# Two modulation groups of the first layer moved from TensorE to VectorE in a two-layer mLSTM / window-attention encoder

## The chip, the cores and the metric

One core of a Trainium2 chip runs the whole program. The metric is the device time of one execution in microseconds; the median of a few timed runs is what is compared. Beside it stands one profiled execution, from which all shares and durations below are read. TensorE (PE) does matrix products, VectorE (DVE) and ScalarE (ACT) elementwise work, GpSimd (POOL) some elementwise work, and SyncE (SP) issues nearly all transfers.

## What is computed

Two sequences, of 256 and 512 rows with 1024 features each, go through two layers and a final norm. Each layer first makes a modulation vector for each sequence, 6 x 1024 numbers, from that sequence's conditioning vector `c`:

```python
mod = jax.nn.silu(c) @ adaln_w[l] + adaln_b[l]
sh1, sc1, g1, sh2, sc2, g2 = [t[:, None, :] for t in jnp.split(mod, 6, axis=-1)]
h = rmsnorm(x, norm_g[l, 0]) * (1 + sc1) + sh1
y = mlstm_mixer(h, ...)            # layer 0;  swa_mixer in layer 1
x = x + g1 * y
h = rmsnorm(x, norm_g[l, 1]) * (1 + sc2) + sh2
x = x + g2 * conv_ffn(h, ...)
```

The mLSTM mixer of layer 0 has 4 heads. Each head projects queries, keys and values (256 wide each), forms decayed scores in both time directions, and sums values by them. An output gate (a sigmoid of a fourth projection) multiplies the heads' results before the output projection.

## The kernel before

**Layout.** Features lie on partitions, the 768 rows of both sequences along the free axis. Products are kept accurate by splitting each operand into a high and a low float32r part (ScalarE casts the high part, VectorE subtracts for the low part, `fp_copy_split`, L271 to L279), and taking three products (`whi` with `zh`, `whi` with `zl`, `wlo` with `zh`).

**Loads.** A weight piece of 128x1024 numbers (512 KB) is fetched by SyncE into one of 5 rotating buffers called `raw` (L282 to L285), in one queue in order. ScalarE and VectorE make `whi` and `wlo` from it, three buffers each. The matrices for the modulation pass through the same 5 `raw` buffers.

**The order on each engine** is made when the program is built: the instructions are traced in the order of the Python code, and a scheduler with a model of the time puts them in a fixed order for each engine, by that order and by when their inputs are expected. It is not changed at run time: an engine whose next instruction waits does nothing else.

**The modulation.** Layer 0's 48 chunks of 128 numbers are called columns 0 to 47 here, layer 1's are columns 48 to 95; eight columns make a group of 1024 numbers.

- Groups 0 and 1 of layer 0 are made on TensorE at the very start (`adaln`, L418).
- Groups 2 to 5 of layer 0 are made on TensorE in the heads' shadow by `adaln_g` (L479): 8 loads of 512 KB, 32 small fp32 matrix products in four bursts of 8 (`silc`, 32 columns wide, is the moving side's partner; the products of one burst use four column strips of the array), one VectorE and one ScalarE copy, two transposes, two VectorE adds of the bias, and for group 4 two VectorE operations that make the gain. It is a generator with 8 stops (`yield`) in each group.
- All 48 columns of layer 1 are made on VectorE by `adaln_v` (L521), from the transposed matrix `adaln_t`: for each column one load of 512 KB, and for each of the two sequences one multiply-and-sum over 128x1024 numbers (L538), which the profile shows as an instruction named CUSTOM_DVE_ANT_0 and a short read of the sum. It is a generator with one stop before the first column and one after each column; the next column's load is issued one step early.

**Who steps the generators.** `first` (L1720) puts the four `adaln_g` in `self.fillp` and `adaln_v` in `self.fill`, and `mlstm` (L664) steps them between its own instructions with `self.step` (L306). `fillp` is stepped in heads 1, 2 and 3 only: after each of the 4 weight pieces of queries and keys (L768), after rows tiles 1, 3 and 5 of the values (L783), and twice ahead of each sequence's output products (L850): 4 + 3 + 4 = 11 times a head, 33 in all. `fill` is stepped 3 times in head 0 (L781), 6 + 3 times in head 1, 8 + 3 times in each of heads 2 and 3 (L765, L781), and 16 times in the loop of the output gate behind the heads (L892): 50 in all.

**The stretch in question** is from the second half of head 2 to the end of the gate's loop. In each head TensorE does four projections for queries and keys, the scores, the values' projection (`gemmN`, L349), and the output products (L859 to L867); the gate's loop (L885 to L896) is 16 projections. Behind it stand the output projection (`out_proj`, L604) and the feed-forward layer, which read layer 0's groups 2 to 5; layer 1 reads its own columns hundreds of microseconds later.

Of the kernel before, what the change touches and what calls it, by code (L numbers as in the profile page):

```python
# [16 lines left out]
P = 128  # L17
D = 1024
# [163 lines left out]
class Net:  # L182
# [122 lines left out]

    def step(self, gen, n=1):  # L306
        for _ in range(n):
            next(gen, None)

    def gemmT(self, w, q):  # L310

# [206 lines left out]
                    self.cst(NG + (2 * l + i) * 8, 8), ALU.add, ALU.mult,  # L518
                )

    def adaln_v(self, l, pool):  # L521

        nc = self.nc
        stt = nc.vector.scalar_tensor_tensor
        row = pool.tile([P, 2, 1024], F32, name="crow")
        nc.sync.dma_start(row, self.crow.to_broadcast([P, 2, 1024]))
        junk = pool.tile([P, 1024], F32, name="junk")
        mod = self.mod[l]
        fetch = lambda j: self.raw(self.io["adaln_t"][j])
        nxt = fetch(0)  # L530
        yield
        for j in range(48):
            w, nxt = nxt, fetch(j + 1) if j < 47 else None
            with ExitStack() as order:
                if j == 0:
                    order.enter_context(self.tc.issue_after(self.opened.ins))
                for s in range(2):
                    nc.vector.tensor_tensor_reduce(  # L538
                        out=junk, in0=w, in1=row[:, s], scale=1.0, scalar=self.cst(AB + 48 * l + j),
                        op0=ALU.mult, op1=ALU.add, accum_out=mod[:, j, s : s + 1],  # L540
                    )
            i = {15: 0, 39: 1}.get(j)
            if i is not None:
                for s in range(2):
                    stt(
                        self.gain[l][i][:, :, s], mod[:, j - 7 : j + 1, s], 1.0,
                        self.cst(NG + (2 * l + i) * 8, 8), ALU.add, ALU.mult,
                    )
            yield
# [54 lines left out]
    def out_proj(self, u0, act, xt, l, apply):  # L604
# [21 lines left out]
        if not self.begun:  # L626
            first = [next(todo) for _ in range(2)]
            todo = chain(first, todo)
            for i, (z, c, w) in enumerate(first):
                self.product(self.bank[2 + i][:, :H], w, act, 0, H, range(KC - 1))  # L630
                self.begun[i] = KC - 1
# [268 lines left out]
    def opening(self, xt, gw, raws, sinks):  # L900
# [73 lines left out]
        with self.tc.manual_schedule(engines={eng.PE, eng.Activation, eng.DVE}):  # L974
# [36 lines left out]
            def first(c):  # L1011
# [3 lines left out]
                return t  # L1015

            ts = {0: first(0)}
            for c in range(KC):
                if c + 1 < KC:
# [418 lines left out]
    def head(self, u0, last_tile, pool, urows, mark, early):  # L1438
# [64 lines left out]
        def factor():  # L1503
            step()
            wc[1], low = split(ra[1])
            late.append(low)
# [3 lines left out]
        next(first)  # L1510
        late.pop()()
        second = self.outset(pa(), wa[1], rows[1][0], step)
        next(second)
        next(first, None)
        step()
        third = self.outset(pa(), ahead[0], urows[1][:, 0])
        next(third)
# [202 lines left out]
    def first(self, pool):  # L1720

        x = self.io["x"]
        xt = self.load_x(x, RANGES[:1])
        ada = self.adaln(0, 0)
        steps = lambda n: [next(ada, None) for _ in range(n)]
        Norm(self, xt, RANGES[0], self.scaled).run()
        steps(4)
        self.load_x(x, RANGES[1:2], xt)
        steps(2)
        Norm(self, xt, RANGES[1], self.scaled).run()  # L1730
        narrow = self.stg.tile([P, 1024], F32, tag="raw", name=self.nm("raw"), bufs=5)[:, : 16 * KC]
        self.nc.sync.dma_start(narrow, self.io["wg"])
        steps(2)
        gates = [self.stg.tile([P, 1024], R, tag=t, name=self.nm(t), bufs=3) for t in ("whi", "wlo")]
        for t in gates:
            self.nc.gpsimd.memset(t.bitcast(F32), 0.0)
        hi, lo = (t.rearrange("p (j m) -> p j m", m=32)[:, :, 0:4] for t in gates)
        self.fp_copy_split(hi, lo, narrow.rearrange("p (j m) -> p j m", m=4))
        self.fillp = chain(*(self.adaln_g(0, grp) for grp in range(2, 6)))
        self.fill = self.adaln_v(1, pool)  # L1740
        act = self.mlstm(pool, gates, xt)
        for _ in chain(self.fillp, self.fill):
            pass
        return act
# [5 lines left out]
def _colpack(a):  # L1750

    a = a.reshape(a.shape[:-1] + (-1, P))
    return np.moveaxis(a, -1, 0).reshape(P, -1)


def _unit_T(w):

    return w.reshape(KC, P, 2, P).transpose(1, 2, 0, 3).reshape(P, 2048)


def _unit_N(w):

    return w.reshape(KC, P, 256).transpose(1, 0, 2).reshape(P, 2048)


def _unit_D(w):

    return w.reshape(2, P, 2, 512).transpose(1, 2, 0, 3).reshape(P, 2048)
# [14 lines left out]
def _shape_constants():  # L1783
    kc = np.zeros((P, NKC), np.float32)
    kc[:, ID : ID + P] = np.eye(P, dtype=np.float32)
    s = np.arange(P)[:, None]
    t = np.arange(P)[None, :]
    kc[:, MF : MF + P] = np.where(s > t, BIG, 0.0)
    kc[:, MB : MB + P] = np.where(s < t, BIG, 0.0)
    b = _buckets()  # L1790
    kc[b, OH + 510 - np.arange(511)] = 1.0
    rel = 255 - np.arange(511)
    kc[32, OH : OH + 511] = np.where(np.abs(rel) > WINDOW, -BIG, 0.0)
    return kc


def _pack(inp):
    arr = {}
    xs = np.concatenate([inp["x_prompt"][0], inp["x_sample"][0]], axis=0)
    arr["x"] = np.ascontiguousarray(xs.T.reshape(KC, P, T).transpose(1, 0, 2))  # L1800
    cst = np.zeros((P, NCST), np.float32)
    cst[:, NG : NG + 32] = _colpack(inp["norm_g"])
    cst[:, AB : AB + 96] = _colpack(inp["adaln_b"])
    cw = inp["ffn_conv_w"].reshape(DEPTH, 3, 44, P)
    cst[:, CW : CW + 264] = cw.transpose(3, 0, 2, 1).reshape(P, 264)
    cst[:, CB : CB + 88] = _colpack(inp["ffn_conv_b"])
    cst[:, HG : HG + 8] = _colpack(inp["mlstm_head_g"].reshape(1, D))
    cst[:, FG : FG + 8] = _colpack(inp["final_g"])
    cst[:, SK : SK + 16] = inp["attn_sink"][0][None, :]
    bg = inp["mlstm_b_gate"][0].reshape(2, 2, 4)  # L1810
    for d in range(2):
        for ty in range(2):
            cst[32 * d : 32 * d + 4, BG + ty] = bg[d, ty]
    c = np.stack([inp["c_sample"][0], inp["c_prompt"][0]], axis=1)
    cst[:, CT : CT + 16] = c.reshape(KC, P, 2).transpose(1, 0, 2).reshape(P, 16)
    arr["cst"] = cst
    arr["kc"] = _shape_constants()
    w = np.empty((N_UNITS, P, 2048), np.float32)
    wi = inp["mlstm_w_in"][0]
    for h in range(4):  # L1820
        for i in range(3):
            f = _unit_N if i == 2 else _unit_T
            w[U_MIN + 3 * h + i] = f(wi[:, i * D + h * 256 : i * D + (h + 1) * 256])
        w[U_MIN + 12 + h] = _unit_T(wi[:, 3 * D + h * 256 : 3 * D + (h + 1) * 256])
    wg = wi[:, 4 * D :].reshape(D, 2, 2, 4).transpose(0, 2, 1, 3).reshape(KC, P, 16)
    arr["wg"] = np.ascontiguousarray(wg.transpose(1, 0, 2).reshape(P, KC * 16))
    wa = inp["attn_w_in"][0]
    w[U_AIN] = _unit_T(wa[:, 1024:1280])
    w[U_AIN + 1] = _unit_N(wa[:, 1280:1536])
    for u in range(4):  # L1830
        cs = slice(u * 256, (u + 1) * 256)
        w[U_AIN + 2 + u] = _unit_T(wa[:, cs])
        w[U_MOUT + u] = _unit_T(inp["mlstm_w_out"][0][:, cs])
        w[U_AOUT + u] = _unit_T(inp["attn_w_out"][0][:, cs])
    for l in range(DEPTH):
        for p in range(NPART):
            u = U_FFN + (l * NPART + p) * 3
            w[u] = _unit_T(inp["ffn_w_up"][l][:, p * 256 : (p + 1) * 256])
            w[u + 1] = _unit_T(inp["ffn_w_up"][l][:, FF + p * 256 : FF + (p + 1) * 256])
            w[u + 2] = _unit_D(inp["ffn_w_down"][l][p * 256 : (p + 1) * 256])  # L1840
    arr["w"] = w
    arr["adaln_w"] = np.ascontiguousarray(inp["adaln_w"][:1])
    arr["adaln_t"] = np.ascontiguousarray(inp["adaln_w"][1].T).reshape(48, P, D)
    arr["crow"] = np.ascontiguousarray(c.T.reshape(16, P))
    arr["rel_bias"] = np.ascontiguousarray(inp["rel_bias"])
    return arr
# [25 lines left out]
```

## Time and profile before

| what | before |
|---|---|
| median of 3 timed runs | 1807.8 us (1804.55 to 1808.11) |
| the profiled execution, its own time | 1808.25 us |
| its span in the trace | 1806.4 us |
| granted TensorE clock in it | 0.996 |
| ScalarE busy | 887.8 us (49%) |
| GpSimd busy | 488.2 us (27%) |
| HBM read | 176.77 MB |

The span is from the first to the last instruction of the program; the 1.85 us between it and the execution's own time lie around it. A TensorE product is shown with its latency: in a run of products of 256 columns each lasts 0.28 us, and the next begins 0.12 us later, so products overlap in the trace and TensorE looks busy wherever one follows another. What it can be made to do faster is read from the distance of the starts.

### The profile page before, as it was taken

Reading aid. Unit: us, or ns where it says so; the run is one execution under the profiler, and the core shown is the slowest. Engines: PE = TensorE matmul, PEld = TensorE weight load, DVE = VectorE, ACT = ScalarE, POOL = GpSimd, SP = SyncE. Lnnn points to the kernel's source line nnn. Section 1 sums busy time; section 2 is a strip of 40 time slices with the busy share of each in tenths; the row PEclk is TensorE's granted clock in tenths of the full one; section 3 lists DMA queues with packets and bytes.
Section 4 is the critical chain, followed back from the end, with each engine's and each line's share of the span. In section 5 each row is a group of like instructions: output and inputs, shape, how many; then the busy total and the mean of one; then the engine's idle time right before and its main releaser. Section 6 shows DMA issues by size and latency. Waiting matters only on the chain.

```text
span 1806.4 us, 28907 instructions
## 1 busy us (share of the span) xinstructions
PE 1773.1 (98%) x11206; PEld 1644.4 (91%) x11206; DVE 1384.8 (77%) x2219; ACT 887.8 (49%) x1789; POOL 488.2 (27%) x397
## 2 busy tenths in 40 slices
PE   7999999999999999999999999999999999999998
PEld 4988888889998999999999999889989999999997
DVE  4876777895799778777777867767998777777877
ACT  4544433444565444444444657665564444444443
POOL 3000000031024333333331313320144333333323
PEclk9999999999999999999999999999999999999999
DMA  9344665656212222222223331234122222222212
GB/s 360 98 140 135 196 207 180 215 180 219 71 59 71 62 67 71 70 71 71 67 64 94 106 93 42 60 92 138 48 82 71 71 71 71 70 70 71 70 36 71
DMA packets 64997, 185.08 MB, mean 102 GB/s; under 512 B 6247, under 2 KB 24839, under 8 KB 64732
## 3 DMA queue, kind: packets, MB, share of 16 engines
q1 hardware_dynamic: 64284, 182.72, 31.3%
q8 instruction: 88, 1.44, 0.3%
q10 hardware_dynamic: 576, 0.52, 0.1%
q14 instruction: 49, 0.40, 0.1%
HBM read 176.77 MB, written 6.44 MB: 101 GB/s over the span
## 4 chain that ended last, share of the span: by engine, by line
PE 87%; DVE 5%; DMA 3%; ACT 3%; issue 1%; POOL 1%; SPq 0%; DVEq 0%; ACTq 0%; POOLq 0%
PE ps L269 28%; PE pa L269 24%; PE ps L1350 11%; PE ps L1351 10%; PE ps L1353 10%; DMA raw<-in_adaln_t_dram 1%; PE pa L1189 1%; DVE junk L538 1%; DMA slab<-in_adaln_w_dram 1%; DVE wlo L276 1%; PE pa L1350 0%; PE pa L1351 0%; PE pa L1353 0%; ACT zh L1301 0%; DMA raw<-in_adaln_w_dram 0%
## 5 line engine op out<-in xcount | busy, mean ns | idle before, releaser
L275 ACT CAST whi<-raw 128x1024 fp32r<-128x1024 f32 (+1 forms) x231 | 241.0, 1045 | 339.0 <-PE pa L269 144.4
L276 DVE TENSOR_TENSOR wlo<-raw,whi 128x1024 fp32r<-128x1024 f32 (+1 forms) x231 | 312.6, 1354 | 119.1 <-ACT whi L275 116.8
L269 PE MATMUL pa<-slab,whi 128*128 128x256 f32 (+1 forms) x1280 | 307.6, 335 | 0.0
L269 PEld LDWEIGHTS pa<-slab,whi 128*128 128x128 f32 x1280 | 222.2, 188 | 21.6 <-DVE slab L602 0.4
L602 DVE SCALAR_TENSOR_TENSOR slab<-pa,mod,slab 128x256 f32<-128x256 f32 (+1 forms) x320 | 187.2, 603 | 62.7 <-PE pa L269 62.6
L269 PE MATMUL pa<-slab,wlo 128*128 128x512 f32 (+1 forms) x640 | 205.7, 334 | 0.0
L269 PE MATMUL ps<-zh,whi 128*128 128x256 f32 (+1 forms) x560 | 188.1, 337 | 0.3 <-ACT zh L948 0.3
L269 PE MATMUL ps<-zl,whi 128*128 128x256 f32 (+1 forms) x560 | 183.6, 330 | 0.5 <-DVE zl L563 0.5
L269 PE MATMUL ps<-zh,wlo 128*128 128x256 f32 (+1 forms) x560 | 181.7, 330 | 0.0
L1350 PE MATMUL ps<-zh,whi 128*128 128x384 f32 x504 | 172.6, 342 | 3.8 <-ACT nt L1421 2.0
L269 PE MATMUL ps<-slab,whi 128*128 128x384 f32 (+2 forms) x704 | 172.0, 329 | 0.9 <-DVE slab L276 0.5
L1351 PE MATMUL ps<-zl,whi 128*128 128x384 f32 x504 | 169.9, 337 | 0.8 <-DVE zl L1307 0.8
L1353 PE MATMUL ps<-zh,wlo 128*128 128x384 f32 x504 | 169.1, 336 | 0.0
L538 DVE CUSTOM_DVE_ANT_0 junk<-raw,crow,cstt 128x1024 f32<-128x1024 f32 x96 | 125.2, 1305 | 25.1 <-DMA raw<-in_adaln_t_dram 24.5
L1386 POOL TENSOR_TENSOR raw<-raw,raw 128x512 f32<-128x512 f32 x40 | 53.8, 1344 | 319.4 <-DVE wlo L276 246.3
L269 PEld LDWEIGHTS pa<-slab,wlo 128*128 128x128 f32 x640 | 120.4, 188 | 13.2 <-DVE wlo L276 0.4
L1602 POOL TENSOR_TENSOR slab<-slab 128x772 f32<-128x772 f32 x44 | 86.5, 1969 | 163.7 <-DVE slab L1590 150.5
L1589 DVE SCALAR_TENSOR_TENSOR slab<-slab,cstt,slab 128x771 f32<-128x771 f32 x88 | 105.4, 1200 | 26.5 <-ACT slab L1587 26.4
L269 PEld LDWEIGHTS ps<-slab,whi 128*128 128x128 f32 x704 | 122.5, 188 | 3.4 <-ACT whi L275 0.9
L269 PEld LDWEIGHTS ps<-zh,whi 128*128 128x128 f32 x560 | 106.8, 191 | 12.8 <-issue 3.5
L269 PEld LDWEIGHTS ps<-zl,whi 128*128 128x128 f32 x560 | 106.8, 191 | 9.5 <-DVE zl L563 0.7
L269 PE MATMUL ps<-slab,wlo 128*128 128x384 f32 (+2 forms) x352 | 114.8, 328 | 0.1
(301 smaller groups left out, 4286.8 us busy)
## 6 DMA issues: line engine op xcount, KB each, us to landing
raw<-in_w_dram SPq DMA_DIRECT2D x208, 512.0 KB, 3.7
raw<-in_adaln_t_dram SPq DMA_DIRECT2D x48, 512.0 KB, 4.2
raw<-in_adaln_w_dram SPq DMA_DIRECT2D x36, 512.0 KB, 4.5
slab<-in_x_dram SPq DMA_DIRECT2D x12, 512.0 KB, 7.2
slab<-in_adaln_w_dram SPq DMA_DIRECT2D x11, 512.0 KB, 9.2
slab<-mrows SPq DMA_DIRECT2D x8, 384.0 KB, 6.3
xs<-slab SPq DMA_DIRECT2D x6, 512.0 KB, 3.6
bt<-brow SPq DMA_DIRECT2D x16, 192.0 KB, 3.1
```

Of the source, the lines that this page charges most:

```text
L269: self.nc.tensor.matmul(out, lhsT, rhs, start=start, stop=stop)
L275: nc.scalar.copy(hi, src)
L276: return nc.vector.tensor_tensor(lo, src, hi.bitcast(F32), ALU.subtract)
L538: nc.vector.tensor_tensor_reduce(out=junk, in0=w, in1=row[:, s], scale=1.0, scalar=self.cst(AB + 48 * l + j), op0=ALU.mult, op1=ALU.add, a ...
L602: return self.nc.vector.scalar_tensor_tensor(x, o, self.mod[l][:, gc + c, q : q + 1], x, ALU.mult, ALU.add)
L1189: nc.tensor.transpose(pp[:, ks], b.t[:, e, ks], self.ident)
L1350: mm(o, wh[:, k], hi[k], start=start and k == 0, stop=False, skip_group_check=True)
L1351: mm(o, wh[:, k], lo[k], start=False, stop=False, skip_group_check=True)
L1353: mm(o, wl[:, k], hi[k], start=False, stop=k == 3, skip_group_check=True)
L1386: tt(q[0], q[2], q[0], ALU.subtract)
L1589: stt(y[:, 1:], u[:, :-1], w(0), y[:, 1:], ALU.mult, ALU.add)
L1602: nc.gpsimd.tensor_tensor(y, y, yrow[:, j], ALU.mult)
```

## The change

`adaln_v` takes a list of columns of both layers instead of a layer. It now makes columns 48 to 63 (layer 1's first two groups), then 32 to 47 (layer 0's last two groups), then 64 to 95. `fillp` keeps the two `adaln_g` of groups 2 and 3. A step that finds `fillp` at its end steps `fill` instead. The packed transposed matrix holds both layers (on the host, before the run); columns 32 to 47 are loaded from it, and not as groups 4 and 5 from the other matrix.

```diff
     def step(self, gen, n=1):
         for _ in range(n):
-            next(gen, None)
+            if next(gen, self) is self and gen is self.fillp:
+                next(self.fill, None)
...
-    def adaln_v(self, l, pool):
+    def adaln_v(self, columns, pool):
...
-        mod = self.mod[l]
-        fetch = lambda j: self.raw(self.io["adaln_t"][j])
+        fetch = lambda i: self.raw(self.io["adaln_t"][columns[i]])
         nxt = fetch(0)
         yield
-        for j in range(48):
-            w, nxt = nxt, fetch(j + 1) if j < 47 else None
+        for i, at in enumerate(columns):
+            w, nxt = nxt, fetch(i + 1) if i + 1 < len(columns) else None
+            l, j = divmod(at, 48)
+            mod = self.mod[l]
             with ExitStack() as order:
-                if j == 0:
+                if i == 0:
                     order.enter_context(self.tc.issue_after(self.opened.ins))
...
-        self.fillp = chain(*(self.adaln_g(0, grp) for grp in range(2, 6)))
-        self.fill = self.adaln_v(1, pool)
+        turned = range(32, 48)
+        self.fillp = chain(*(self.adaln_g(0, grp) for grp in range(2, 4)))
+        self.fill = self.adaln_v([*range(48, 64), *turned, *range(64, 96)], pool)
...
-    arr["adaln_t"] = np.ascontiguousarray(inp["adaln_w"][1].T).reshape(48, P, D)
+    arr["adaln_t"] = np.ascontiguousarray(inp["adaln_w"].transpose(0, 2, 1)).reshape(96, P, D)
```

The body of a column's step is unchanged:

```python
for s in range(2):
    nc.vector.tensor_tensor_reduce(
        out=junk, in0=w, in1=row[:, s], scale=1.0, scalar=self.cst(AB + 48 * l + j),
        op0=ALU.mult, op1=ALU.add, accum_out=mod[:, j, s : s + 1],
    )
```

## The prediction

> **What bounds the kernel now.** First the page: busy shares, and the chain that ended last.
>
> ```profile
> span 1806.4 us, 28907 instructions
> PE 1773.1 (98%) x11206; PEld 1644.4 (91%) x11206; DVE 1384.8 (77%) x2219; ACT 887.8 (49%) x1789; POOL 488.2 (27%) x397
> PE 87%; DVE 5%; DMA 3%; ACT 3%; issue 1%; POOL 1%; SPq 0%; DVEq 0%; ACTq 0%; POOLq 0%
> ```
>
> TensorE carries 87% of the chain, so work taken from it is worth its full time, as long as nothing else becomes late. VectorE's 77% is a mean; what the change does to it is decided where the work goes. So, second, busy time by stretch (columns: length, then PE, PEld, DVE, ACT, POOL, then clock and DMA). The cuts are: values and outputs of head 2, queries and keys of head 3, its scores and values, its outputs with the first gate products, and the rest of the gate's loop.
>
> ```profile
> 250.00:283.80 33.80, 33.80 (x277) 29.98 (x274) 20.36 (x54) 13.66 (x44) 0.00 (x0) 1.00 0.65 218
> 283.80:316.30 32.50, 32.13 (x191) 26.57 (x189) 26.02 (x54) 9.09 (x21) 3.64 (x2) 1.00 0.53 171
> 316.30:342.60 26.30, 26.30 (x218) 22.49 (x217) 23.23 (x46) 13.42 (x27) 0.00 (x0) 1.00 0.65 211
> 342.60:370.80 28.20, 28.20 (x195) 24.91 (x193) 23.07 (x51) 12.09 (x36) 4.74 (x4) 1.00 0.65 209
> 370.80:422.20 51.40, 51.40 (x302) 45.56 (x302) 42.31 (x64) 21.41 (x43) 20.07 (x14) 1.00 0.61 193
> ```
>
> TensorE has no hole in any of them but 0.4 us in the second. VectorE's idle time is 13.4, 6.5, 3.1, 5.1 and 9.1 us: 37.2 us over 172.2 us.
>
> **What TensorE loses.** Third, the order of time around one burst of the modulation's products, and the transposes of one group in the chain.
>
> ```profile
> 179.26 0.28 PE L269 MATMUL ps<-whi,zl 128*128 128x256 f32 x1
> 179.38 0.28 PE L269 MATMUL ps<-wlo,zh 128*128 128x256 f32 x1
> 179.59 1.07 PE L269 MATMUL ps<-raw,silc 128*32 128x256 f32 x16
> 180.59 0.39 PE L269 MATMUL ps<-whi,zh 128*128 128x256 f32 x1
> 180.81 0.28 PE L269 MATMUL ps<-whi,zl 128*128 128x256 f32 x1
> 304.99 0.22 PE ps L507 x2
> ```
>
> Ordinary products start 0.12 us apart. From the one at 179.38 to that at 180.81 there are 1.43 us where two such steps would take 0.24, so a burst costs 1.19 us. All 256 such records are 16 bursts, four to a group; two groups are 8 bursts, 9.5 us, and four transposes of 0.11 us, 0.4 us: **10.0 us less on TensorE**. Of the loads, 16 of 512 KB go and 16 of 512 KB come, on the same queue through the same buffers: no byte more or less.
>
> The Trainium skill, Perfetto Trace Analysis, Identifying the Most-Contended Engine, says that matmul busy time is a bad measure of TensorE and that weight-load time should be read. Here weight loads fill 26.57 of 32.5 us and 22.49 of 26.3 us. Read so, TensorE had some 15% to spare there and the saving would be nearer 8.5 us; the starts 0.12 us apart speak for the full 10.0.
>
> **What VectorE gets.** The price of a column, from a stretch with 11 of them (22 sums and 22 reads), and the adds and copies that go.
>
> ```profile
> 268.00:348.00 80.00, 28.35 (x44) 1.00 0.60 199
> L502 DVE COPY sb<-ps 128x128 f32<-128x128 f32 x4 | 1.1, 285 | 3.5 <-PE ps L269 3.5
> L512 DVE TENSOR_TENSOR mod<-ps,cstt 128x8 f32<-128x8 f32 x8 | 0.9, 159 | 0.2
> ```
>
> 28.35 / 11 = 2.58 us a column; 16 columns are 41.3 us. Two copies and four adds go, 1.0 us (the gain of group 4 is only moved). So 40.3 us come to an engine with 37.2 us free in the stretch where they land, and the stretch itself is to become 10 us shorter.
>
> **Where they land** follows from counting steps. `fillp` has 33 steps: 11 in each of heads 1 to 3. Two groups use 16; the 17th finds the end and steps `fill`, as do the rest. The 17th is at values tile 3 of head 2. So head 2 gets 6 more columns (2 in the values, 4 ahead of the outputs), head 3 gets 11 more (4 in queries and keys, 3 in the values, 4 ahead of the outputs), and the gate's loop has 14 instead of 15. The bursts that go lie in the same stretches: 3, 1, 3 and 1. VectorE's balance, stretch by stretch (idle before, less columns at 2.58, less TensorE time that goes, plus copies and adds that go):
>
> - values and outputs of head 2: 13.4 - 15.5 - 3.6 = -5.7 us;
> - queries and keys of head 3: 6.5 - 10.3 - 1.4 + 0.5 = -4.7, in all -10.4;
> - its scores and values: 3.1 - 7.7 - 3.6 = -8.2, in all -18.6;
> - its outputs: 5.1 - 10.3 - 1.4 + 0.5 = -6.1, in all -24.7;
> - rest of the gate's loop: 9.1 + 2.6 = +11.7, in all -13.0.
>
> A deficit is no loss yet: what VectorE had made ahead of need can come later. Ahead at 342.6 were two weight pieces of the gate and one column of its loop:
>
> ```profile
> 334.27 1.28 DVE L538 CUSTOM_DVE_ANT_0 junk<-raw,crow,cstt 128x1024 f32<-128x1024 f32 x1
> 337.19 1.23 DVE L276 TENSOR_TENSOR wlo<-raw,whi 128x1024 fp32r<-128x1024 f32 x1 [0.58 <-ACT whi L275]
> 341.65 1.23 DVE L276 TENSOR_TENSOR wlo<-raw,whi 128x1024 fp32r<-128x1024 f32 x1 [0.31 <-ACT whi L275]
> ```
>
> That is 2.6 + 2.5 = 5.1 us. What TensorE needs at once has little slack, as head 3's values show: their low weights end at 318.85 + 1.23 = 320.08, and the first product with them starts at 322.07.
>
> ```profile
> 318.85 1.23 DVE L276 TENSOR_TENSOR wlo<-raw,whi 128x1024 fp32r<-128x1024 f32 x1 [1.63 <-ACT whi L275]
> 322.07 0.28 PE L269 MATMUL ps<-wlo,zh 128*128 128x256 f32 x1
> ```
>
> So 18.6 - 5.1 - 2.0 = 11.5 us of wait at TensorE by the end of head 3's values. VectorE will not be busy without a gap either. In the view of groups the sums already wait for their loads:
>
> ```profile
> L538 DVE CUSTOM_DVE_ANT_0 junk<-raw,crow,cstt 128x1024 f32<-128x1024 f32 x96 | 125.2, 1305 | 25.1 <-DMA raw<-in_adaln_t_dram 24.5
> ```
>
> 24.5 us for 48 columns, about 0.5 us each; the 13 new columns up to there would add 6.6 us, none if a backlog lets loads run ahead. I take 2.5, estimated between the ends 0 and 6.6 and nearer to 0, since VectorE would be the late one: **a wait of 14 us**. Behind it the outputs and the gate's loop have room: the low weights made at 364.98 are used from 380.07 on, 14 us later, against the 6.1 us of the outputs and the 5.1 us owed.
>
> ```profile
> 364.98 1.21 DVE L276 TENSOR_TENSOR wlo<-raw,whi 128x1024 fp32r<-128x1024 f32 x1
> 380.07 0.40 PE L269 MATMUL ps<-zh,whi 128*128 128x512 f32 x1
> ```
>
> That columns do hold up TensorE is seen once already, in head 0:
>
> ```profile
> 114.53 1.28 DVE L538 CUSTOM_DVE_ANT_0 junk<-raw,crow,cstt 128x1024 f32<-128x1024 f32 x1
> 115.73 1.13 DVE L810 SCALAR_TENSOR_TENSOR E<-slab,aT,kct 128x128 f32<-128x128 f32 x4
> 116.38 0.94 ACT L816 ACTIVATE E<-E 128x256 f32<-128x256 f32 x2 [1.12 <-DVE E L810]
> 117.86 0.82 PE L720 MATMUL pa<-kct,slab 36*128 36x36 f32 x6 [3.05 <-ACT slab L278]
> ```
>
> A sum stands ahead of the decay terms, ScalarE waits in order for these, and TensorE stands for 3.05 us. Behind a new wait of VectorE in head 3 the same are queued: the low weights, the evictions and the score tiles that the next products need.
>
> **The sum**, against the profiled execution's own time: 1808.25 - 10.0 + 14 = 1812.2. The median of the runs is 0.45 lower, so **1812** is said for the median. Other work is left as it is: layer 0's columns 32 to 47 come 17th to 32nd of the 64, the last of them early in head 3, and are needed behind the gate's loop.
>
> **The rivals.**
>
> *TensorE is spared (faster).* What the columns take of the fifth stretch now:
>
> ```profile
> 370.80:422.20 51.40, 23.61 (x34) 1.00 0.61 193
> ```
>
> The order on VectorE is fixed when the program is built, and a column is wanted by nobody near. If the scheduler lets weights, evictions and scores pass, the columns slide into the gate's loop, whose balance is +11.7 us and which has 14 us of slack. Then only the last deficit counts, 13.0 us against that slack: a wait of 0 to 6 us, 1798 to 1804. For it: in the fifth stretch VectorE is 82% busy with 23.6 us of columns and TensorE has no hole. Against it: the order follows the code where inputs are ready, the columns stand ahead of the evictions and products of their tile in the code, and their loads come first in the queue. It decides from some 10 us of columns passed over. One thing would then cost more: sums beside GpSimd's products stretch.
>
> ```profile
> 369.97 1.63 POOL L895 TENSOR_TENSOR sg<-sg,slab 128x512 f32<-128x512 f32 x1
> 370.50 2.19 DVE L538 CUSTOM_DVE_ANT_0 junk<-raw,crow,cstt 128x1024 f32<-128x1024 f32 x1
> ```
>
> 2.19 for 1.28 us; four columns pushed there would pay up to 0.9 us for each of 8 sums, 7 us at most, within the slack. The Trainium skill, Trainium Architecture, The Big Picture, What this means for kernel authors, says that VectorE and GpSimd share a port under an exclusive lock; these two rows agree.
>
> *The five load buffers run dry (slower still).* A load of the old groups was given back by TensorE after one burst of 1.07 us; a column's load is held until VectorE has made both sums. In the view of waits SyncE already stood for VectorE:
>
> ```profile
> SPq L284 <- DVE wlo L276: 91.5, 23, 20.6
> SPq L284 <- DVE mod L538: 82.1, 30, 4.4
> ```
>
> If a backlog holds the buffers, the weights queue behind the columns, each weight pays load, cast and subtraction in turn, and nothing of the deficit is hidden: 24.7 us of wait, 1823, with the 6.6 us of load waits up to 1829. It decides once three of five buffers hold waiting columns.
>
> *TensorE had room (less saved).* By the weight-load reading above 8.5 us are saved and the 14 us stay: 1813.3; were half of the bursts hidden, 5 us saved and 1817.
>
> *The change does less than it says:* a column not stepped in time would be drained behind the gate's loop. The steps are 50 + 17 = 67 and 65 are needed, so none is.
>
> **How the numbers follow.** A measurement here tells 0.2%, 3.6 us, from no change: faster is below 1804.2, slower above 1811.4. The forecast, a wait between 8 and 22 us (1806 to 1820), gets 0.46, of it 0.30 slower and 0.16 the same. Columns that slide get 0.38, of it 0.33 faster and 0.05 the same. Dry buffers get 0.10, slower; TensorE with room 0.06, half slower, half the same. Together: faster 0.33, the same 0.24, slower 0.43. The range leaves out the last few us at both ends: 1799 to 1823. The forecast's own is 1806 to 1820.
>
> **What would show it.** Right: VectorE above 95% busy from about 260 us to the end of head 3, holes at TensorE in head 3 of some 14 us that end with low weights, evictions or score tiles of VectorE, none in the gate's loop, and 10 us fewer bursts. Wrong: TensorE without holes and the gate's loop ending about 10 us earlier than 422 us (the columns slid); holes that end with weight loads (dry buffers); columns later than the gate's loop; or a time below 1798, which nothing here explains.

## The result, and the profile after

| what | before | after |
|---|---|---|
| median of the timed runs | 1807.02 us | 1819.88 us |
| ratio to before, 95% interval | | 1.0073 (1.0053 to 1.0092) |
| profiled execution, its own time | 1808.25 us | 1819.9 us |
| span in the trace | 1806.4 us | 1818.0 us |
| granted TensorE clock | 0.996 | 0.990 |
| first product of the output projection (end of the gate's loop) | 422.2 us | 433.5 us |

The change makes the kernel 0.7% slower, some 13 us. In the traces 11.3 of the 11.65 us between the two profiled executions have come up by the end of layer 0's gate loop (last row of the table); from there on the two run alike. One of the four timed runs after took 9836.56 us, the other three 1819.66 to 1819.9; it is left out of the ratio. The top of the page and the group of the sums, after:

```profile
span 1818.0 us, 28708 instructions
PE 1768.3 (97%) x11074; PEld 1647.1 (91%) x11074; DVE 1421.5 (78%) x2277; ACT 886.7 (49%) x1787; POOL 486.2 (27%) x397
PE 86%; DVE 5%; ACT 3%; DMA 2%; issue 2%; POOL 1%; SPq 0%; POOLq 0%; DVEq 0%; ACTq 0%
L540 DVE CUSTOM_DVE_ANT_0 junk<-raw,crow,cstt 128x1024 f32<-128x1024 f32 x128 | 169.7, 1326 | 15.6 <-DMA raw<-in_adaln_t_dram 14.3
```

The page alone hides it: the shares moved by a point, and the change is at work in a tenth of the span. The sums rose from 96 to 128 at the same price (1305 ns before, 1326 now), while their waits for loads fell from 24.5 to 14.3 us: with a backlog on VectorE the loads are there in time. So the same stretches as before, for the kernel after (length, then PE, PEld, DVE, ACT, POOL, clock, DMA), with the end of the gate's loop added:

```profile
250.00:283.80 33.80, 33.80 (x241) 31.84 (x240) 31.70 (x71) 12.74 (x38) 0.00 (x0) 1.00 0.60 191
283.80:316.30 32.50, 29.10 (x160) 24.65 (x158) 30.99 (x61) 9.62 (x26) 2.72 (x2) 0.95 0.54 173
316.30:342.60 26.30, 22.93 (x188) 22.72 (x189) 25.98 (x57) 12.50 (x31) 0.00 (x0) 0.99 0.45 139
342.60:370.80 28.20, 26.00 (x156) 23.03 (x155) 25.65 (x51) 13.40 (x39) 7.88 (x5) 0.95 0.55 169
370.80:422.20 51.40, 41.69 (x217) 36.18 (x217) 48.17 (x69) 14.04 (x24) 11.03 (x8) 0.87 0.56 175
422.20:433.50 11.30, 11.30 (x75) 10.30 (x74) 11.23 (x15) 5.08 (x9) 4.46 (x4) 1.00 0.78 230
```

VectorE went from 60 to 88% busy to 91 to 99%, and TensorE, which had stood for 0.4 us in all, now stands for 2.2 to 9.7 us in each stretch from the second to the fifth. The granted clock fell too, to 0.87 in the fifth. The view of TensorE's waits between 45 and 560 us (total, times, longest) says on what:

```profile
PE ps L269 <- ACT whi L275: 11.8, 3, 9.7
PE pa L722 <- ACT slab L278: 2.6, 1, 2.6
PE pa L269 <- ACT slab L875: 2.4, 1, 2.4
PE pa L740 <- ACT slab L875: 2.2, 1, 2.2
PE pa L740 <- ACT slab L736: 1.8, 1, 1.8
```

The second row is the hole of head 0 that was there before. The others are new. By the distances of the products' starts there are eight new holes, 20.0 us: 10.2 us in seven between 286 and 368 us (head 3), each of 2.5 us or less, and one of 9.9 us in the gate's loop, at 370.6 us. That one is read from two views. First SyncE's row of issues around it (start, length, what, how many):

```profile
342.87 3.65 SPq L284 DMA_DIRECT2D raw<-in_w_dram  x2
348.89 23.21 SPq L284 DMA_DIRECT2D raw<-in_adaln_t_dram  x8
375.91 0.33 SPq L284 DMA_DIRECT2D raw<-in_w_dram  x1
```

Eight columns' loads stand in a row before the gate's next weight piece, four from the steps ahead of head 3's outputs and four from the gate's loop. Each waits for a buffer that VectorE frees with a column. The chain of work of the same kernel shows the end of it:

```profile
374.60 1.27 DVE junk L540
375.87 0.02 DVE mod L540
...
375.91 3.54 DMA raw<-in_w_dram
...
379.47 1.05 ACT whi L275
...
380.57 19.48 PE ps L269 x94
```

The last number of a column is read at 375.87, the weight's load is issued in the buffer that this frees, lands 3.5 us later, is cast, and only then does TensorE go on. The wait is put down to ScalarE (`whi`), which was idle; VectorE's sums are the cause.

**An account of the 11.3 us.** Bursts and transposes that went, with a wait of 0.4 us beside one of them: -14.8 us (the section on the reasons says why not -10.0). Holes: +20.0. Products that took longer right behind holes, against the same products before: +5.3 (the last section). Together +10.5; the other 0.8 us are what is left of several waits of under 0.4 us, and of 0.9 us that this execution was already ahead at 241 us, in front of the first burst that goes.

### The profile page after: what moved, and what is told of

Its sections match the earlier page's. It is cut to its first block, busy times and chain, and to the rows that moved or that the text cites. A ratio compares the mean times of both kernels' runs of the same rounds, so it can differ in the third digit from the quotient of the medians.

```text
span 1818.0 us, 28708 instructions
## 1 busy us (share of the span) xinstructions
PE 1768.3 (97%) x11074; PEld 1647.1 (91%) x11074; DVE 1421.5 (78%) x2277; ACT 886.7 (49%) x1787; POOL 486.2 (27%) x397
## 4 chain that ended last, share of the span: by engine, by line
PE 86%; DVE 5%; ACT 3%; DMA 2%; issue 2%; POOL 1%; SPq 0%; POOLq 0%; DVEq 0%; ACTq 0%
PE ps L269 28%; PE pa L269 24%; PE ps L1352 10%; PE ps L1353 10%; PE ps L1355 10%; DVE junk L540 1%; PE pa L1191 1%; DMA raw<-in_adaln_t_dram 1%; DMA raw<-in_w_dram 1%; DVE wlo L276 1%; DMA slab<-in_adaln_w_dram 0%; PE pa L1352 0%; PE pa L1353 0%; PE pa L1355 0%; DMA raw<-in_adaln_w_dram 0%
## 5 line engine op out<-in xcount | busy, mean ns | idle before, releaser
L540 DVE CUSTOM_DVE_ANT_0 junk<-raw,crow,cstt 128x1024 f32<-128x1024 f32 x128 | 169.7, 1326 | 15.6 <-DMA raw<-in_adaln_t_dram 14.3
L269 PEld LDWEIGHTS pa<-slab,wlo 128*128 128x128 f32 x640 | 120.4, 188 | 13.2 <-DVE wlo L276 0.4
L269 PEld LDWEIGHTS ps<-zh,wlo 128*128 128x128 f32 x560 | 106.5, 192 | 10.8 <-DVE wlo L276 1.0
```

The lines of the kernel that those rows point to most:

```text
L269: self.nc.tensor.matmul(out, lhsT, rhs, start=start, stop=stop)
L540: nc.vector.tensor_tensor_reduce(out=junk, in0=w, in1=row[:, s], scale=1.0, scalar=self.cst(AB + 48 * l + j), op0=ALU.mult, op1=ALU.add, a ...
```

## The experiments

The theory: VectorE's work falls due in head 2's outputs and head 3, where VectorE has no room for it, and TensorE pays the deficit. The rivals: the loads and their place in SyncE's queue; an effect of the removal itself. The first four runs share their runs of the kernel before (median 1807.61 us), the next four theirs (1808.33), the last three theirs (1807.01).

| run | median, us | ratio to before (95%) | holes up to the end of the gate's loop | end of the gate's loop |
|---|---|---|---|---|
| every second step to the columns | 1802.92 | 0.9970 (0.9959 to 0.9982) | 11.9 | 416.0 |
| sums cut to 64 of 1024 | 1803.98 | 0.9974 (0.9963 to 0.9986) | 7.5 | 417.4 |
| no loads for the moved columns | 1815.74 | 1.0042 (1.0028 to 1.0056) | 18.8 | 431.4 |
| one group moved | 1810.73 | 1.0015 (1.0005 to 1.0024) | 7.8 | 425.7 |
| columns mostly in head 1 | 1795.51 | 0.9931 (0.9916 to 0.9946) | 5.9 | 408.7 |
| none ahead of head 3's outputs | 1815.06 | 1.0043 (1.0027 to 1.0060) | 11.5 | 422.1 |
| two groups left out | 1792.66 | 0.9913 (0.9898 to 0.9928) | 0 | 407.0 |
| a gate weight loaded early | 1819.06 | 1.0061 (1.0046 to 1.0076) | 23.3 | 434.0 |
| columns evenly in heads 1 and 2 | 1790.89 | 0.9914 (0.9899 to 0.9929) | 1.0 | 403.7 |
| left out, 20 sums more | 1795.37 | 0.9933 (0.9916 to 0.9949) | 0 | 406.4 |
| left out, 10 sums more | 1793.28 | 0.9926 (0.9912 to 0.9941) | 0 | 407.1 |

Holes are those over 0.4 us from 119 us on, by the distances of the products' starts, a burst's own cost not counted. Diffs are against the changed kernel unless said.

**Every second step to the columns.**

```diff
     def step(self, gen, n=1):
         for _ in range(n):
+            if gen is self.fillp:
+                self.calls = getattr(self, "calls", 0) + 1
+                if self.calls % 2 == 0:
+                    next(self.fill, None)
+                    continue
```

> The same 16 columns are on VectorE, but every second step of the product generator goes to the columns from head 1 on, so each of heads 1 to 3 gets 5 or 6 of them (some 14 us of VectorE a head, against 23.6, 18.0 and 21.0 us idle there before) and TensorE's 16 bursts are spread over all three heads. Theory of the place (VectorE overflows only because the columns bunch in the second half of head 2 and in head 3): no holes at TensorE, the 10 us of bursts are gained, 1797 to 1801 us. Rival, the total (the columns are too dear for VectorE wherever they stand): 1812 us or more.

1802.92 us: the same work on every engine, 17 us less than the changed kernel, by the order alone. It is above the 1797 to 1801 us of the theory, and holes of 11.9 us are left where none was expected: the largest, 4.1 us in head 3, where the transposes of group 3 waited for VectorE's copy. Nor do all 17 us come from the stretch in question. The scheduler also ordered head 0 otherwise: its hole of some 3 us and the slower products behind it, another 3 us, are gone. Without these 6 us (a difference, not a run) the kernel would be about level with the one before. In the kernel before, in this one, and in the fastest one below, from 100 to 130 us (length, then PE, PEld, DVE, ACT, POOL, clock, DMA):

```profile
100.00:130.00 30.00, 26.77 (x136) 22.79 (x135) 25.73 (x57) 15.12 (x35) 0.10 (x1) 0.89 0.29 98
100.00:130.00 30.00, 29.22 (x173) 25.39 (x172) 27.88 (x61) 14.41 (x33) 0.10 (x1) 1.00 0.35 114
100.00:130.00 30.00, 30.00 (x172) 26.08 (x171) 30.00 (x62) 14.97 (x32) 0.10 (x1) 1.00 0.47 150
```

**Sums cut short.**

```diff
+                    m = 64 if l == 0 else 1024
...
-                        out=junk, in0=w, in1=row[:, s], scale=1.0, ...
+                        out=junk[:, :m], in0=w[:, :m], in1=row[:, s, :m], scale=1.0, ...
```

> As the changed kernel, but each sum of the moved columns takes 64 of its 1024 numbers (the rest of those sums is left out); all loads and their order stay. Theory of VectorE's time (the sums of 1.28 us make the backlog): the holes go, 1797 to 1801 us. Rival, the loads (512 KB column loads in SyncE's queue ahead of the weights cost the time, whatever is computed from them): 1808 us or more.

1803.98 us, 16 us less than the changed kernel, with all its loads in their places. VectorE's time is the larger part of the price. It isn't all: 11 us stay above the kernel that leaves both groups out. The eight loads in a row before a gate weight are there too. Here as in the changed kernel they are columns of layer 1, which keep their full sums (the moved columns are the 17th to 32nd and are loaded from 208 to 275 us in the changed kernel); they only come sooner:

```profile
326.28 0.33 SPq L284 DMA_DIRECT2D raw<-in_w_dram  x1
327.42 27.13 SPq L284 DMA_DIRECT2D raw<-in_adaln_t_dram  x8
358.34 0.33 SPq L284 DMA_DIRECT2D raw<-in_w_dram  x1
```

TensorE's waits for weights fell all the same: 0.6 us for low ones and 0.5 us for high ones, against 9.7 us in one wait. The largest hole, 4.0 us at 357 us, ended with an eviction (L876). So the row of loads alone does not make the long hole; it takes a VectorE that is behind.

**Loads left out, sums kept.**

```diff
-        fetch = lambda i: self.raw(self.io["adaln_t"][columns[i]])
+        fetch = lambda i: row[:, 0] if columns[i] < 48 else self.raw(self.io["adaln_t"][columns[i]])
```

> As the changed kernel, but the moved columns are summed from the resident conditioning row instead of loaded columns: their 16 loads of 512 KB are left out, the 32 full sums stay. If the holes come through the five load buffers (columns hold them, weights queue behind): the 9.9 us hole ahead of the gate's third weight piece mostly goes and the time falls to 1798 to 1806 us. If VectorE's own queue is late without them: 1810 to 1820 us.

1815.74 us, 4 us less than the changed kernel. The sixteen loads are the smaller part, and 7.0 of the 10.2 us of holes in head 3 stay. A hole of 11.8 us in the gate's loop, ended by `whi`, stays too. That does not clear the queue there, as was expected of this run: the row ahead of the gate's third weight piece consists of layer 1's columns, which are still loaded.

```profile
346.48 24.98 SPq L284 DMA_DIRECT2D raw<-in_adaln_t_dram  x8
374.01 0.33 SPq L284 DMA_DIRECT2D raw<-in_w_dram  x1
```

**One group moved.**

```diff
-        turned = range(32, 48)
-        self.fillp = chain(*(self.adaln_g(0, grp) for grp in range(2, 4)))
+        turned = range(40, 48)
+        self.fillp = chain(*(self.adaln_g(0, grp) for grp in range(2, 5)))
```

> Only group 5 is moved, groups 2 to 4 stay on TensorE: 8 columns, all stepped in head 3, and 5 us of bursts less. By a proportional cost: half of the 12 us, 1813 us. By a balance that must first use up VectorE's idle 15 us of head 3 against 21 us of columns: a wait of 5 to 10 us against the 5 us saved, 1807 to 1812 us. If the load buffers are the cause the hole at the gate's weights stays, some 5 to 10 us long.

1810.73 us, 3 us above before. One group is a loss too, a quarter of the loss of two: holes of 7.8 us against 20.0. The largest, 5.3 us at 365 us, ended with an eviction (L875) and not with a gate weight.

**Columns mostly in head 1.** As the first experiment, with the condition

```diff
+                if self.calls in (1, 2, 4, 5, 7, 8, 10, 11, 17, 19, 20, 21, 22, 23, 27):
```

> As e1_spread, with the columns put where VectorE was idle before: 8 in head 1, 5 in head 2 (4 of them ahead of its outputs), 2 in head 3's queries and values, none ahead of head 3's outputs; TensorE's two groups take the other steps, 3, 6 and 8. Theory of the place: no hole above 2 us, 1797 to 1801 us, below e1_spread. If head 1 (23.6 us idle, 20.6 us of columns and 2 bursts less) overflows instead, a hole of some us comes there: 1801 to 1805 us. Theory of the total price: as e1_spread or above.

1795.51 us: faster than both kernels, and lower than expected. The whole computation is done. Some 6 us are again head 0's. The theory's "no hole above 2 us" failed: one of 5.2 us at 279 us stands ahead of head 3's first products, and a row of column loads precedes its weight, as above, nine here:

```profile
252.73 24.97 SPq L284 DMA_DIRECT2D raw<-in_adaln_t_dram  x9
277.87 0.33 SPq L284 DMA_DIRECT2D raw<-in_w_dram  x1
```

The condition names 15 of the 33 steps, and the two groups on TensorE use 16 of the other 18. So the last two steps ahead of head 3's outputs find them at their end and step columns after all. The same holds for the last version below, with another 15.

**None ahead of head 3's outputs.**

```diff
-                self.step(self.fillp, 2 if h else 0)
+                self.step(self.fillp, 2 if h in (1, 2) else 0)
```

> As the changed kernel, but the 4 columns ahead of head 3's outputs aren't stepped there; they follow in the gate's loop and two of them behind it. If the 9.9 us hole is made by the 8 column loads that stand in SyncE's queue ahead of the gate's third weight piece, 4 fewer of 2.6 us each take it away: 1808 to 1812 us. If VectorE is late by the sum of its work whatever the order, the hole comes back later in the loop: 1816 us or more.

1815.06 us, 5 us less than the changed kernel, between the two theories. TensorE's waits between 119 and 435 us:

```profile
PE ps L269 <- ACT whi L275: 5.2, 3, 3.6
PE pa L269 <- ACT slab L875: 2.4, 1, 2.4
PE pa L740 <- ACT slab L875: 2.2, 1, 2.2
PE ps L269 <- DVE wlo L276: 1.2, 3, 0.6
```

The larger holes of head 3 are as they were, but for the last. That of 9.9 us is gone, but 3.7 us stand at the end of the loop, with slower products behind them. Four column loads now precede the gate's third weight piece, not eight. I read this as somewhat over half of the 9.9 us for the queue of loads at that place and the rest for work still owed; the run moved four columns' sums along with their loads, so it does not show the split.

**Two groups left out** (against before):

```diff
-        self.fillp = chain(*(self.adaln_g(0, grp) for grp in range(2, 6)))
-        self.fill = self.adaln_v(1, pool)
+        self.nc.vector.memset(self.mod[0][:, 32:48], 0.0)
+        self.nc.vector.memset(self.gain[0][1], 0.0)
+        self.fillp = chain(*(self.adaln_g(0, grp) for grp in range(2, 4)))
+        self.fill = self.adaln_v(range(48, 96), pool)
```

> Groups 4 and 5 of layer 0 are left out on both engines (zeros stand for them), so this is the change with only its removals. The prediction's first term says 10.0 us less than before, 1797 to 1799 us. If TensorE had room under the bursts: 1800 to 1804 us.

1792.66 us: the removal (the groups' 16 loads go with it) is worth 15.7 us, not 10.0, and the loop ends 15.2 us earlier. From 119 us to there TensorE has no hole.

**A gate weight loaded early.**

```diff
+                if h == 3:
+                    self.pre[U_MIN + 13, 0] = self.load(U_MIN + 13, 0)
...
-            yield h, self.early.pop((u, h), None) or self.split(self.load(u, h))
+            yield h, self.early.pop((u, h), None) or self.split(self.pre.pop((u, h), None) or self.load(u, h))
```

> As the changed kernel, but the load of the gate's third weight piece is issued ahead of head 3's four last columns, so it stands in front of the 8 column loads and not behind them. All column work and every other load stay. If the place in SyncE's queue makes the 9.9 us hole: it goes or falls below 3 us, 1808 to 1813 us. If VectorE's backlog makes it: the hole moves to the fourth piece, 1816 us or more.

1819.06 us, no gain. SyncE's row shows where the hole went (three weight loads now come first, then ten columns):

```profile
343.10 6.42 SPq L285 DMA_DIRECT2D raw<-in_w_dram  x3
350.46 31.41 SPq L285 DMA_DIRECT2D raw<-in_adaln_t_dram  x10
384.90 0.33 SPq L285 DMA_DIRECT2D raw<-in_w_dram  x1
```

The next piece stands behind ten columns, and TensorE for 12.6 us at 377 us. Moving a load past the backlog only chooses which weight pays.

**Columns evenly in heads 1 and 2.** The condition is now

```diff
+                if self.calls in (1, 2, 4, 5, 7, 8, 10, 11, 13, 15, 17, 19, 21, 24, 27):
```

> As the best version so far (the moved columns taken at the earlier steps: eight in head 1, five in head 2, two in head 3), but the five of head 2 are spread over its steps (one in queries and keys, two in the values, two ahead of the outputs) and head 3 still gets two. That version had one large hole, 5.2 us at 279 us, ahead of head 3's first product: eight column loads in a row stood before its weight piece. Theory (VectorE's work has to be placed stretch by stretch, and the steps ahead of the outputs are the worst place, since four columns in a row stand there before the next weight piece): the hole shrinks to under 2.5 us and the time is 1791 to 1795, 0.989 to 0.993 of the kernel before. Rival (the place of single columns does not matter any more, only their sum up to the end of head 3): no change, 1795 to 1797.

1790.89 us, at the lower end of what was expected (1791) and the fastest of all: 16 us under the kernel before, 29 under the changed one, with the whole computation done. TensorE's only wait between 119 and 435 us, and VectorE in the stretch from head 1 to head 2's values, in this kernel and then in the one before:

```profile
PE ps L269 <- DVE wlo L276: 0.8, 1, 0.8
```

```profile
119.00:250.00 131.00, 131.00 (x930) 118.55 (x929) 118.75 (x263) 58.42 (x157) 5.49 (x5) 1.00 0.53 165
```

```profile
119.00:250.00 131.00, 131.00 (x915) 114.20 (x914) 94.83 (x213) 56.98 (x151) 4.47 (x5) 0.98 0.49 157
```

VectorE had 131.0 - 94.8 = 36.2 us idle there before, and the better version uses 23.9 of them without a hole at TensorE. That is the room that the change did not use: by its order the first moved step falls in head 2's values, where the stretch ends. The ratio is that of the kernel that leaves the groups out, but this does not make the sixteen columns free. Head 0's hole and the slower products behind it, some 6 us, are gone here and not there, and the loop ends only 3.3 us earlier than there. So the columns cost some 3 us (a difference, not a run), and part of the tie is luck. Why the new order closes head 0's hole wasn't looked into.

**Twenty and ten more sums where nothing else is late** (against the kernel that leaves the groups out; for ten, 6 in place of 11):

```diff
-                for s in range(2):
+                for s in [0, 1] * (11 if i == 47 else 1):
```

> The kernel that leaves groups 4 and 5 of the first layer out on both engines (1792.7 us, no holes from head 1 to the end of the gate's loop), with one column of the gate's loop summed eleven times in place of once: 20 sums of 1.28 us, 25.6 us of VectorE in one piece, the output as with one. Groups 4 and 5 stay zero. Theory A (a hole costs its length and then a slower TensorE: in the changed kernel the products behind a hole of 9.9 us took 1.8 times their time for some 6 us): one hole of some 8 to 12 us in the gate's loop, and the products in the 4 to 6 us behind it take about 1.8 times their time, which costs 2 to 2.6 us more than the hole; the total grows by the hole and these 2 to 2.6 us, 1802 to 1808. Theory B (a hole costs its length; the slower products in the changed kernel came from the columns' loads and sums beside them): products behind the hole at their usual 0.23 us, and the total grows by the hole alone.

> The same kernel (groups 4 and 5 left out), the column summed six times in place of once: 10 more sums, 12.8 us of VectorE in one piece. Weights in the gate's loop of the kernel before are made 14 us ahead of their use. Theory A (that reserve covers a backlog up to its size): no hole over 1 us, no slower products, 1791 to 1794. Theory B (the backlog reaches TensorE at once through another work of VectorE, such as the split of the gated outputs): a hole of 2 us or more, and the time 1795 or more.

Ten more sums, 12.8 us of VectorE: 1793.28 us and no hole. The reserve covers them. Twenty more, 25.6 us: 1795.37 us, and one hole of 2.3 us, not of 8 to 12, and not in the loop but just behind it, at 413.7 us. The sums didn't stay in one piece; VectorE's order put the loop's weights and splits between them, so the backlog was carried along to its end. The hole was too small by far to test its length, but it did tell the two theories of slower products apart. The products of 384 columns in the 4 us behind it, and products of the same kind, at about the same time, without the extra sums:

```profile
L269 PE MATMUL ps<-slab,whi 128*128 128x384 f32 x9 | 3.6, 488 | 2.1 <-DVE slab L276 2.1
L269 PE MATMUL ps<-slab,wlo 128*128 128x384 f32 x5 | 2.4, 481 | 0.0
```

```profile
L269 PE MATMUL ps<-slab,whi 128*128 128x384 f32 x17 | 4.3, 337 | 0.0
L269 PE MATMUL ps<-slab,wlo 128*128 128x384 f32 x8 | 2.7, 337 | 0.0
```

They cost 1.8 us on top of the 2.3, though no column is loaded there any more and the last extra sum ends 1 us after the hole. Between the end of the loop and the next part's first product the kernel is 4.0 us longer than the one without the sums.

## Why the prediction came out as it did

The direction and the range were right: 1812 forecast, 1799 to 1823, 1819.88 measured, and the cause is in the main the one forecast, a VectorE that can't take 16 columns in that stretch. The number owes something to luck: both terms of the sum were too small, 10.0 for 14.8 and 14 for 25.3, and part of the errors cancelled. Nor was the longest hole of the kind that was forecast: of the 20.0 us, 13.2 ended with a weight piece, 9.9 of them with one that had been loaded late, which the prediction had named as a sign against itself.

*The bursts, 10.0 us: too small.* The price of a burst of 16 products was read at 179 us and multiplied by 8, on the claim that all 256 records are 16 bursts. Those that go do not lie in bursts of 16. The kernel before, in order of time (start, length, what):

```profile
331.27 0.28 PE L269 MATMUL ps<-wlo,zh 128*128 128x256 f32 x1
331.48 0.62 PE L269 MATMUL ps<-raw,silc 128*32 128x256 f32 x4
332.04 0.38 PE L269 MATMUL ps<-whi,zh 128*128 128x256 f32 x1
...
342.02 0.63 PE L269 MATMUL ps<-raw,silc 128*32 128x256 f32 x6
342.58 2.17 PE L269 MATMUL pa<-slab,PT 128*128 128x258 f32 x16
344.69 0.63 PE L269 MATMUL ps<-raw,silc 128*32 128x256 f32 x4
```

From 261.9 us on the 128 records lie in 14 pieces of 2 to 16. A piece of 4 costs 332.04 - 331.27 - 0.12 = 0.65 us up to the next product, and some 0.1 more in that product's own step (0.22 for 0.12 us from 180.59 on, in the prediction's rows); the whole 16 there cost 1.09 and 0.1 in the same way. By the starts, pieces of 2 to 6 cost 0.64 to 0.65 us and pieces of 10 to 16 cost 1.07 to 1.09 us. So half of the price and more is the switch, not the products. The 14 pieces come to 12.96 + 1.38 = 14.3 us, with the transposes 14.8, and the run without the groups gave 15.7 in the median. The reading by the weight-load share (8.5 us), one of the rivals, went the wrong way: the room that PEld seems to leave is nowhere saved.

*VectorE's balance, -5.7, -4.7, -8.2: right in place and kind.* VectorE is 94, 95 and 99% busy in these stretches. The share alone would prove nothing: without the groups it is 31.7 of 34 us from 250 us on and 30.7 of the next 32, and TensorE has no hole, since VectorE there works ahead of need (15 sums from 250 to 284 us, against 7 in the kernel before). But cutting the moved sums short gave back 16 us, and spreading them over heads 1 to 3 gave back 17 to 29, some 6 of these in head 0, so this is shown and not only argued. The holes in head 3 ended as forecast, 6.9 us with evictions (L875, L736) and the rest with weights. They came to 10.2 us, below the 14; whether the lead and the slack were worth more than was put in isn't shown.

*"Behind it the outputs and the gate's loop have room": the step that failed.* The 14 us between low weights and their use were read in a kernel without a backlog, where they are real: 12.8 us of sums cost nothing, 25.6 us some 4. But the step weighed only VectorE's time. What the change brings ahead of the loop is also eight loads in SyncE's queue, and a weight behind them has no lead at all: it is issued when the eighth column is nearly done. Of the 14 us nothing was left, and a hole of 9.9 us came where "none in the gate's loop" was written.

*The load gaps, 2.5 us: not needed.* The sums' waits for loads fell from 24.5 to 14.3 us, so the backlog hid them, as the lower end had it. Without the moved columns' loads the time fell by some 4 us.

*The rival "five load buffers run dry" had the mechanism of that hole*, weights that queue behind columns, and it was given 0.10. Its price, 24.7 us for all of the deficit, is close to the 25.3 us of holes and slower products that were paid, and its 1823 lies nearer to the result than 1812. As the whole cause it falls: two thirds of head 3's holes ended with evictions, most of them stay without the moved columns' loads, and short sums took the gate weight's wait away with the row of eight loads in place. No run kept VectorE's work and took the row itself away. Queue and backlog are one thing here: a load waits for a buffer, the buffer for VectorE.

*Columns that slide* (0.38) did not. They kept their place ahead of head 3's outputs. The argument against them, that the order follows the code, held.

*Nothing in the sum* stood for the slower products behind a hole, some 5 us.

What stays open: how the 9.9 us split exactly between queue and deficit (6 and 4 by the run without steps ahead of the outputs, which also moves four columns), and whether a sixth load buffer would help, which wasn't tried.

## What to carry to other kernels

Work that nobody near waits for should be put where the engine that takes it is idle, and its loads not in a row ahead of a load that something waits for: with the same instructions, the place of sixteen columns made 29 us of difference, from 1.0073 to 0.9914 of the time before (some 6 us of it because the new order also closed a hole in head 0). An order that is made for one stretch can move another, so compare the whole trace before the gain is put down to the stretch. A lead read in the old kernel ("made 14 us ahead") is a lead only as long as the loads behind it are issued as early; list what the change puts ahead of them in the queue. When bursts are priced, count their pieces in the trace and not in the code, for a piece of 2 records cost 0.64 us here and one of 16 cost 1.09.

## What the runs showed of the hardware

A hole costs more than its length. One group of products in the 10 us behind the 9.9 us hole, the changed kernel, and in the kernel that leaves the groups out, in the same window (381 to 391 us):

```profile
L269 PE MATMUL ps<-zl,whi 128*128 128x512 f32 x8 | 4.1, 511 | 0.0
```

```profile
L269 PE MATMUL ps<-zl,whi 128*128 128x512 f32 x9 | 3.5, 391 | 0.0
```

By the distance of starts, products take 1.8 times their usual step for the first 6 us behind that hole, and then the usual one: some 2.5 us lost. Eight holes from 3.7 to 12.6 us, one in each of eight kernels, were followed by 2 to 6 us of steps 1.7 to 1.9 times as long, 1.0 to 2.9 us lost; those of 2.3 to 2.5 us mostly by 1.4 to 1.8 us, but one, with the gate weight loaded early, by under 0.3; and those of 1.0 to 1.8 us mostly by under 0.3, but one of 1.7 us, with every second step to the columns, by 1.6. So the length of the hole alone does not set the price. The granted clock shows it in the kernel with 20 more sums, behind its hole of 2.3 us, in the first and the second 4 us:

```profile
416.10:420.10 4.00, 3.91 (x14) 3.92 (x15) 4.00 (x10) 2.83 (x4) 0.00 (x0) 0.60 0.87 234
420.10:424.10 4.00, 4.00 (x24) 4.00 (x23) 2.10 (x5) 1.05 (x1) 0.00 (x0) 0.98 0.79 259
```

The Trainium skill, TensorE: Matmul & The Clock Gate, What's actually happening, says that the clock falls to half after an idle window of about 3.4 us and comes back after as much sustained work. Half the clock and some microseconds of recovery agree with these rows; the length does not quite, since 2.3 us of idle time were enough here, and one hole of 2.4 us was not.
